# Instance norm on one core: tiles of 48 KiB per partition in four slots, two small parts first and three last

## The chip, the core and the metric

The kernel runs on one core of a Trainium2 chip. Times are device microseconds (us) of the whole program; the profile's span of the same execution is about 1.7 us shorter. The kernel before takes 1248.05 us, the median of three runs (1247.97 to 1248.34). The profile of before is of a run of its own, 1247.95 us.

Engines are named as in the profile: PE is TensorE, DVE is VectorE, ACT is ScalarE, POOL is GpSimd, SP is SyncE. Loads are issued by SP and run in queue q1; stores are issued by ACT and run in queue q10. Both queues run on the same 16 DMA engines.

## The reference

Each of 8 x 64 = 512 instances of 32 x 64 x 64 = 131072 fp32 numbers gets its own mean and variance:

```python
mean = np.mean(x, axis=(2, 3, 4), keepdims=True)
var = np.var(x, axis=(2, 3, 4), keepdims=True)
return ((x - mean) / np.sqrt(var + eps)).astype(np.float32)
```

That is 268.44 MB in and 268.44 MB out, and every number is needed twice on the chip (statistics, then scaling), so each tile stays in SBUF from its load to its store.

## The kernel before

64 tiles of 4 MiB (8 instances, 32 KiB in each of 128 partitions) go through six slots; the last tile is handled as two halves. Per tile, VectorE and ScalarE each sum half, a matmul with a matrix of ones over the partitions of one instance gives the mean, ScalarE squares and sums, a second matmul gives the variance, and the two engines scale half each.

```python
COLS = 8192
SLOTS = 6
FULL = P * COLS // n_elem
ROUNDS = (n_tiles - 1) // SLOTS
...
# on_scalar, per tile
eng.activation(out=unused[:, : 2 * w], in_=t, func=Act.Square,
               bias=a[:, 2:3], accum_out=a[:, 3:4]
)._wait_ge(centred[lane], c1).then_inc(squared[lane], 1)
...
eng.dma_start(out=dst, in_=t)._wait_ge(done[lane], c2).then_inc(stored[lane], 16)
...
# load_all, in the loop: a slot is loaded when its store is through
eng.dma_start(out=slots[s][:], in_=x_t[it * SLOTS + s])._wait_ge(
    stored[s], c16
).then_inc(landed[s], 16)
```

(Cuts are marked with "...".)

## Time and profile before

| what | value | where it is read |
|---|---|---|
| time | 1248.05 us | median of 3 |
| span | 1246.2 us | page |
| DMA queues q1 and q10 | 50.0% and 49.9% of 16 engines' span | page, part 3 |
| ScalarE, VectorE | 79%, 38% | page, part 1 |
| first data packet starts | 2.1 us | packet records |
| idle time of a DMA engine between first and last byte, mean of 16 | 2.1 us | packet records |

The trace has a record of every DMA packet, with start, duration, bytes and queue. A row of one partition is one packet. Packets of one engine follow each other with an overlap of 3 to 4 ns, so they can be chained into 16 engines; where fewer than 16 packets run, an engine is idle. The GB/s of the page count a packet where it starts, so they swing by some per cent from slice to slice; spread over their durations the packets give a flat rate. A packet is called late when its record is over 50 ns longer than the median of its size. The record names no engine, and the chaining is not always unique, so what is said of single engines is good to a packet or two.

### The profile page before, as it was taken

Reading aid. Unit: us, or ns where it says so; the run is one execution under the profiler, and the core shown is the slowest. Engines: PE = TensorE matmul, PEld = TensorE weight load, DVE = VectorE, ACT = ScalarE, POOL = GpSimd, SP = SyncE. Lnnn points to the kernel's source line nnn. Section 1 sums busy time; section 2 is a strip of 40 time slices with the busy share of each in tenths; the row PEclk is TensorE's granted clock in tenths of the full one; section 3 lists DMA queues with packets and bytes.
Section 4 is the critical chain, followed back from the end, with each engine's and each line's share of the span. In section 5 each row is a group of like instructions: output and inputs, shape, how many; then the busy total and the mean of one; then the engine's idle time right before and its main releaser. Section 6 shows DMA issues by size and latency. Waiting matters only on the chain.

```text
span 1246.2 us, 1808 instructions
## 1 busy us (share of the span) xinstructions
PE 76.4 (6%) x260; PEld 65.2 (5%) x260; DVE 468.0 (38%) x325; ACT 986.1 (79%) x410; POOL 1.9 (0%) x11
## 2 busy tenths in 40 slices
PE   0000000000000000000000000000000000000000
PEld 0000000000000000000000000000000000000000
DVE  2344334433334334343343433434334333343331
ACT  5888888887787878778777877787787778878774
POOL 0000000000000000000000000000000000000000
DMA  9999999999999999999999999999999999999998
GB/s 404 421 438 428 430 438 436 428 431 438 435 429 431 438 435 429 431 436 436 429 431 436 436 429 430 438 436 426 433 438 436 426 433 438 435 425 435 438 429 380
DMA packets 18722, 536.90 MB, mean 431 GB/s; under 512 B 2080, under 2 KB 2080, under 8 KB 2080
## 3 DMA queue, kind: packets, MB, share of 16 engines
q1 hardware_dynamic: 9360, 268.44, 50.0%
q10 hardware_dynamic: 9360, 268.44, 49.9%
q14 instruction: 2, 0.02, 0.0%
HBM read 268.44 MB, written 268.44 MB: 431 GB/s over the span
## 4 chain that ended last, share of the span: by engine, by line
ACT 48%; DVE 29%; another core or an unknown queue 13%; PE 6%; issue 1%; DMA 1%; ACTq 0%; DVEq 0%; SPq 0%
ACT unused L113 37%; DVE small L79 18%; DVE slot L95 8%; ACT slot L123 4%; ACT unused L107 4%; PE psum L136 3%; PE psum L143 3%; ACT small L120 1%; ACT L120 1%; DMA slot<-in_x_dram 1%; DVE small L89 1%; DVE small L82 1%; DVE small L92 1%; ACTq L130 0%
## 5 line engine op out<-in xcount | busy, mean ns | idle before, releaser
L113 ACT ACTIVATE unused<-slot,small 128x8192 uint8<-128x8192 f32 (+1 forms) x65 | 456.1, 7016 | 90.2 <-DVE small L82 90.2
L79 DVE TENSOR_REDUCE small<-slot 128x1 f32<-128x4096 f32 (+1 forms) x65 | 283.0, 4353 | 163.7 <-DMA slot<-in_x_dram 163.7
L107 ACT ACTIVATE unused<-slot 128x4096 uint8<-128x4096 f32 (+1 forms) x65 | 231.7, 3564 | 81.9 <-DMA slot<-in_x_dram 76.7
L123 ACT ACTIVATE slot<-slot,small 128x4096 f32<-128x4096 f32 (+1 forms) x65 | 243.7, 3749 | 27.6 <-DVE small L92 27.6
L89 DVE RECIPROCAL small<-small 128x1 f32<-128x1 f32 x65 | 10.6, 164 | 533.8 <-ACT small L120 533.8
L95 DVE TENSOR_SCALAR slot<-slot,small 128x4096 f32<-128x4096 f32 (+1 forms) x65 | 154.7, 2380 | 2.4
L136 PE MATMUL psum<-small,avg 128*128 128x2 f32 x130 | 38.2, 363 | 673.9 <-DVE small L79 548.5
L136 PEld LDWEIGHTS psum<-small,avg 128*128 128x128 f32 x130 | 32.6, 311 | 679.4 <-DVE small L79 552.7
L143 PE MATMUL psum<-small,avg 128*128 128x1 f32 x130 | 38.2, 363 | 480.6 <-ACT unused L113 480.6
L143 PEld LDWEIGHTS psum<-small,avg 128*128 128x128 f32 x130 | 32.7, 312 | 486.1 <-ACT unused L113 486.1
L120 ACT ACTIVATE small<-psum,eps_t 128x1 f32<-128x1 f32 x65 | 17.0, 261 | 37.4 <-PE psum L143 37.3
L82 DVE TENSOR_REDUCE small<-psum 128x1 f32<-128x2 f32 x65 | 10.4, 160 | 62.8 <-PE psum L136 62.8
L107 ACT ACT_TABLE_LOAD x10 | 12.8, 1283 | 10.4 <-ACT slot L123 7.1
L120 ACT ACT_TABLE_LOAD x10 | 12.8, 1283 | 0.2
L107 ACT ACTIVATION_READ_ACCUMULATOR unused<-slot 128x1 f32 x65 | 12.1, 186 | 0.0
L113 ACT ACTIVATION_READ_ACCUMULATOR unused<-slot,small 128x1 f32 x65 | 12.1, 186 | 0.0
L92 DVE TENSOR_TENSOR small<-small 128x1 f32<-128x1 f32 x65 | 10.4, 159 | 2.2
L204 POOL TENSOR_SCALAR_AFFINE_SELECT avg<-avg 128x128 f32<-128x128 f32 x4 | 1.3, 324 | 0.3
L201 POOL MEMSET avg<- 128x128 f32 x2 | 0.4, 204 | 0.5 <-SPq L42 0.5
L246 POOL MEMSET const-bfloat16-1.0<- 128x1 bf16 x1 | 0.1, 101 | 0.0
L246 POOL MEMSET const-uint8-127<- 128x1 uint8 x1 | 0.1, 101 | 0.0
L214 POOL MEMSET eps_t<- 128x1 f32 x1 | 0.1, 99 | 0.0
(2 smaller groups left out, 0.2 us busy)
## 6 DMA issues: line engine op xcount, KB each, us to landing
slot<-in_x_dram SPq DMA_DIRECT2D x63, 4096.0 KB, 53.3
out_dram<-slot ACTq DMA_DIRECT2D x63, 4096.0 KB, 45.3
slot<-in_x_dram SPq DMA_DIRECT2D x2, 2048.0 KB, 55.6
out_dram<-slot ACTq DMA_DIRECT2D x2, 2048.0 KB, 14.7
```

Source lines behind the costliest of these rows:

```text
L79: eng.reduce_sum(out=a[:, 0:1], in_=t[:, :w], axis=mybir.AxisListType.X)._wait_ge(landed[lane], c16).then_inc(summed[lane], 1)
L82: eng.tensor_reduce(out=a[:, 2:3], in_=psum[lane][:, 0:2], axis=mybir.AxisListType.X, op=Alu.add, negate=True,)._wait_ge(meaned[lane], c1) ...
L89: eng.reciprocal(out=a[:, 5:6], in_=a[:, 4:5])._wait_ge(rooted[lane], c1).then_inc(scaled[lane], 1)
L92: eng.tensor_mul(out=a[:, 6:7], in0=a[:, 2:3], in1=a[:, 5:6])._wait_ge(scaled[lane], c1).then_inc(shifted[lane], 1)
L95: eng.tensor_scalar(out=t[:, w:], in0=t[:, w:], scalar1=a[:, 5:6], scalar2=a[:, 6:7], op0=Alu.mult, op1=Alu.add,)._wait_ge(shifted[lane], ...
L107: eng.activation(out=unused[:, w : 2 * w], in_=t[:, w:], func=Act.Identity, accum_out=a[:, 1:2],)._wait_ge(landed[lane], c16).then_inc(sum ...
L113: eng.activation(out=unused[:, : 2 * w], in_=t, func=Act.Square, bias=a[:, 2:3], accum_out=a[:, 3:4],)._wait_ge(centred[lane], c1).then_in ...
L120: eng.activation(out=a[:, 4:5], in_=psum[lane][:, 2:3], func=Act.Sqrt, bias=eps_t[:, 0:1])._wait_ge(varied[lane], c1).then_inc(rooted[lane ...
L123: eng.activation(out=t[:, :w], in_=t[:, :w], func=Act.Identity, scale=a[:, 5:6], bias=a[:, 6:7],)._wait_ge(shifted[lane], c1).then_inc(don ...
L136: eng.matmul(out=psum[lane][:, 0:2], lhsT=avg[n][:], rhs=a[:, 0:2], start=True, stop=True,)._wait_ge(summed[lane], c2).then_inc(meaned[lan ...
L143: eng.matmul(out=psum[lane][:, 2:3], lhsT=avg[n][:], rhs=a[:, 3:4], start=True, stop=True,)._wait_ge(squared[lane], c1).then_inc(varied[la ...
L204: eng.affine_select(out=m[:], in_=m[:], pattern=[[sign * split, n], [0, split]], compare_op=Alu.is_ge, fill=0.0, base=0 if sign < 0 else s ...
```

## The change

The intent: longer rows, so fewer packets and transfers, and shorter ends. A tile now has 48 KiB per partition and holds 12 instances, and there are four slots (4 x 48 = 6 x 32 KiB). 41 such tiles are preceded by two parts of 2 MiB (16 KiB per partition, FRONT) and followed by three. The last three parts use the slot of tile 37 and are loaded when that is stored. The store of the last tile, tile 40, is held until the second of the last three parts has landed. A partition now holds parts of up to two instances' chunks, so sums are kept per third of a tile and brought to instances with masks (four small VectorE operations around each matmul). VectorE takes over the square and sum of one third. The wait of tile 40's store is called the hold below.

```diff
-    COLS = 8192
-    SLOTS = 6
+    CHUNK = 4096
+    THIRDS = 3
+    COLS = THIRDS * CHUNK
+    SLOTS = 4
+    PART = P * CHUNK // n_elem
+    FRONT = 2
+    n_tiles = (n_inst // PART - FRONT) // THIRDS - 1
+    n_parts = n_inst // PART - THIRDS * n_tiles
...
+        eng.tensor_tensor_reduce(
+            out=unused[2][:], in0=chunk[0], in1=chunk[0],
+            scale=1.0, scalar=0.0, op0=Alu.mult, op1=Alu.add,
+            accum_out=column(a, SQUARES, 0),
+        )._wait_ge(moved[lane], c1).then_inc(squared[lane], 1)
...
+        if behind is not None:
+            eng.wait_ge(landed[behind], 16)
+        eng.dma_start(out=dst, in_=t)._wait_ge(done[lane], c3).then_inc(
+            stored[lane], 16
+        )
...
+    AHEAD = SLOTS + n_parts - 2
...
+            if with_target and k == n_tiles - 1:
+                more += (AHEAD,)
...
+    nc.scalar.preload_act_table(Act.Sqrt)
```

## The prediction

> **What bounds the kernel now.** I read the page from the totals down: busy shares, slices, queues, groups, then the waits of the load queue, and last the timeline of the two ends.
>
> ```profile
> PE 76.4 (6%) x260; PEld 65.2 (5%) x260; DVE 468.0 (38%) x325; ACT 986.1 (79%) x410; POOL 1.9 (0%) x11
> DMA  9999999999999999999999999999999999999998
> GB/s 404 421 438 428 430 438 436 428 431 438 435 429 431 438 435 429 431 436 436 429 431 436 436 429 430 438 436 426 433 438 436 426 433 438 435 425 435 438 429 380
> DMA packets 18722, 536.90 MB, mean 431 GB/s; under 512 B 2080, under 2 KB 2080, under 8 KB 2080
> q1 hardware_dynamic: 9360, 268.44, 50.0%
> q10 hardware_dynamic: 9360, 268.44, 49.9%
> ...
> slot<-in_x_dram SPq DMA_DIRECT2D x63, 4096.0 KB, 53.3
> out_dram<-slot ACTq DMA_DIRECT2D x63, 4096.0 KB, 45.3
> ```
>
> No compute engine is full: ScalarE is at 79%. The 16 DMA engines are: nine tenths or more in every slice but the last, and the load queue (q1) and the store queue (q10) fill 50.0% and 49.9% of their time. A tile moves 4 MiB in and 4 MiB out, and at 431 GB/s that takes 8.39 MB / 431 = 19.5 us. A load lands 53.3 us after its issue and a store 45.3 us, which are 2.7 and 2.3 such periods: each queue always holds a transfer behind the running one. ScalarE needs only 7.12 + 3.62 + 3.80 + about 0.9 = 15.4 us of the 19.5.
>
> ```profile
> SPq L185 <- DMA out_dram<-slot: 1048.9, 54, 50.6
> ```
>
> This is the load queue's own wait: loads wait for stores to free slots. It looks like the loss, but costs nothing while earlier loads are still queued, which the 53.3 us say. The chain of waits names ScalarE for 48% for the same reason: it follows semaphores and does not see that the DMA engines are full.
>
> The ends:
>
> ```profile
> 1.03 2.93 SPq L180 DMA_DIRECT2D slot<-in_x_dram  x6
> 13.23 4.42 DVE L79 TENSOR_REDUCE small<-slot 128x1 f32<-128x4096 f32 x1 [13.23 <-DMA slot<-in_x_dram]
> ...
> 1211.81 0.34 ACTq L130 DMA_DIRECT2D out_dram<-slot  x1
> 1222.36 0.34 ACTq L130 DMA_DIRECT2D out_dram<-slot  x1
> 1223.26 1.91 ACT L107 ACTIVATE unused<-slot 128x2048 uint8<-128x2048 f32 x1 [0.93 <-DMA slot<-in_x_dram]
> 1233.70 0.34 ACTq L130 DMA_DIRECT2D out_dram<-slot  x1
> ```
>
> The first 4 MiB land at 13.23; 4.19 MB at 433 GB/s are 9.7 us, so bytes flow from about 3.6 us on. At the end the last half tile lands at 1223.26 and its store is issued 10.4 us later, but earlier stores are still moving: I spread every packet of the trace over its duration and found 16 engines busy in every 2 us bin from 1204 to the end. **Neither end has a hole to close.** The only losses are 3.6 us before the first byte, slow first packets of loads and stores (together 1.5 us per engine), and what a packet costs beyond its bytes.
>
> **What the Trainium skill says.** "DMA: Bandwidth & Descriptors", section "Where 436 GB/s comes from", puts the fabric's ceiling at 435.2 GB/s. The spread packets give 433.2 GB/s over each tenth of the middle: 0.5% below it, so it agrees, and there is no more to win than that half per cent plus the ends. The same page, "Why small descriptors are slow (HBM only)", says that each packet has a small fixed overhead. The packet records agree: 32 KiB take 1213 ns, 16 KiB 611 ns, and twice 611 less 1213 leaves 9 ns; the 4-byte packets that report completion take 9 ns as well. "VectorE: DVE Perf Modes", section "The perf-mode tier table (the rule you actually need)", has tensor_reduce and fp32 tensor_tensor at one element per cycle and fp32 tensor_scalar at two. The trace has 4.42 us for a reduction of 4096 and 2.41 us for the scaling of 4096, so it agrees; I use it to size the new square-and-sum on VectorE. "ScalarE: Activation LUTs", section "What ACT_TABLE_LOAD costs", gives about 1283 ns a load; the page of before has 20 loads of 1283 ns.
>
> **The change part by part.**
>
> *Transfers.* 63 tiles of 4 MiB and two halves become 41 tiles of 6 MiB (48 KiB per partition) and five parts of 2 MiB, two first and three last. Bytes are equal. Per engine, data packets go from (63 + 2) x 8 x 2 = 1040 to (41 + 5) x 8 x 2 = 736, if a 48 KiB row stays one packet as the 32 KiB row does, and completions from 130 to 92. That is 1170 - 828 = 342 fewer. At 9 ns each it is 3.1 us. But neighbouring packets overlap slightly (the durations sum to 16.04 busy engines): at 433.2 GB/s an engine takes 1210.3 ns for 32 KiB, against 1204 ns for the bytes alone (twice the difference of the two sizes), so 6.3 ns for 9/8 of a packet, 5.6 ns each: 342 x 5.6 = **1.9 us**. I take 2.3 us, between the two and nearer the lower.
>
> *VectorE per tile.* Two reductions, 4.42 and about 1.75 (the step from 2282 ns at 2048 to 4419 at 4096 is 1.04 ns an element; 1536 elements); subtracting the mean 2.41; square and sum, estimated from the tier table as a one-element-a-cycle pass at 4.42 plus 0.19 for reading the accumulator; two scalings 4.82; ten small operations of about 0.17. Sum 19.7 us.
>
> *ScalarE per tile.* Sums over 4096 and 2560 elements 3.62 + 2.34, squares 2 x 3.71, scaling 3.80, root 0.26, four accumulator reads 0.75. Sum 18.2 us.
>
> Both lie beside a transfer period of 12.58 MB / 433.2 = 29.0 us. VectorE goes from 38% to about 68%, ScalarE from 79% to about 62%; neither is the bound, so moving work between them is worth nothing in time. All table loads but one go, 19 x 1.28 = 24 us of ScalarE, hidden too.
>
> *Latency of a tile,* landing to store: sums 6.35; masks, matmul and gathering 1.5 (four small operations of 0.2 and a matmul of 0.6); squares 7.8; masks again 1.5; root, reciprocal, shift 0.7; scaling 4.85. Sum 22.7 us, against about 17.4 in before. A slot comes round every 4 x 29.0 = 116 us, leaving 93 us for its load and store, which need 29 each when they share the engines. So both queues stay filled: I expect about 48 us issue to landing for loads and 45 for stores.
>
> *Start.* Part 0 lands near 8.5 us, its store goes out near 19 (10.5 us a part, as the halves in before), is through by about 31, and frees the load of tile 2 near 32. The loads before it are 16 MiB, which with the two small stores last until about 52. No hole. Stores begin 12 us earlier than in before (31.57), but that only reorders bytes: loads already filled the engines.
>
> *End.* Counted from the landing of tile 40: its store is ready at 23; the parts land at 10, 19 and 29, so the hold until the second landed barely waits. Parts compute one after another at about 10.6 us each: stores issued near 34, 45 and 55. Stores already queued last until 34 (tile 39), then 14.5 for tile 40 and 4.8 for each of two parts: 58. The last store's data start about 1.5 us after issue, near 57: covered by about 1 us. I count no hole, but the margin is thin.
>
> *Sum.* 1248.05 - 2.3 = 1245.75; I say **1245.7 us**.
>
> **Rivals.**
> - *A hole at the end.* The margin of 1 us rests on steady queues; if the store backlog is shorter, the engines idle 1 to 4 us before the last parts. For it: 10.6 us a part against 4.8 us of transfer. Against: 6 MiB of tile 40 ahead. Time 1247 to 1249.
> - *Rows of 48 KiB are cut* into 32 + 16 KiB. Then the two data packets of a row cost one fixed part more, and 41 x 128 x 2 / 16 = 656 packets come back per engine: net 314 more than before, +1.8 us, 1250. Nothing in the profile shows a row above 32 KiB; 16 and 32 KiB were both uncut.
> - *VectorE becomes the bound.* It would need the square-and-sum at over three times my estimate (9 us of slack). It would have to exceed 29 us a tile; 30 us would make 41 us more. Unlikely, as known rows make up 15 of the 19.7 us.
> - *Everything hidden, nothing gained.* If the 9 ns overlap wholly with the next packet's reading, only noise is left: 1248.
>
> **Range and chances.** The best case is all 3.1 us and about 1 us at the ends, 1244; the worst likely one a hole of 3 us with little won, 1248.5. I give 1243.7 to 1248.5 for 8 in 10. Over 2% faster would need 1223, below bytes over the ceiling (536.87 MB / 435.2 = 1233.6): 0.01. Over 2% slower needs 1273, a compute-bound or starving loop: 0.03. Within 2%: 0.96.
>
> **What would show it.** Right: DMA nines in all slices, data packets of 48 KiB at about 1815 ns, packets down to about 828 x 16 = 13,250, mean near 432 GB/s, VectorE near 68% and ScalarE near 62%, loads landing after about 48 us and stores after 45, one table load. Wrong: a slice under nine after the first stores or in the last three; packets of 16 KiB at over 1280; a load queue whose wait for stores ends after the previous load landed; a square-and-sum much over 4.6 us; or a per-byte rate that changes with the row length.

## The result, and the profile after

The changed kernel takes **1252.14 us** (median of 4 runs, 1251.42 to 1254.22) beside 1248.14 us of the kernel before: ratio 1.0035, interval 1.0017 to 1.0052. The change is within 2%, as the chances said, but it loses 4 us where 2.3 were to be won, and lies above the range.

The page of the changed kernel, in the same order as for the kernel before:

```profile
PE 55.0 (4%) x184; PEld 46.1 (4%) x184; DVE 804.4 (64%) x722; ACT 764.6 (61%) x441; POOL 2.7 (0%) x15
...
DMA  9999999999999999999999999999999999999997
GB/s 393 427 444 434 427 429 447 430 427 433 444 429 427 446 432 427 433 438 433 429 440 435 432 427 443 435 429 432 441 433 427 440 436 430 430 438 435 433 397 306
DMA packets 13250, 536.89 MB, mean 429 GB/s; under 512 B 1472, under 2 KB 1472, under 8 KB 1472
...
q1 hardware_dynamic: 6624, 268.44, 49.7%
q10 hardware_dynamic: 6624, 268.44, 49.6%
...
L173 DVE CUSTOM_DVE_ANT_0 unused<-slot 128x4096 uint8<-128x4096 f32 x41 | 181.5, 4426 | 1.4
...
slot<-in_x_dram SPq DMA_DIRECT2D x41, 6144.0 KB, 39.9
out_dram<-slot ACTq DMA_DIRECT2D x41, 6144.0 KB, 54.3
slot<-in_x_dram SPq DMA_DIRECT2D x5, 2048.0 KB, 31.6
```

Neither compute engine is the bound (64% and 61%), the packets are as few as predicted, and the DMA row is nines to the last slice. The loss shows in two places only: the last two GB/s figures, 397 and 306 where before had 429 and 380, and the split of the waiting, 39.9 us for a load and 54.3 us for a store.

The timeline of the last 75 us, cut to the last tile and the parts; a bracket is idle time of the engine and what ended it:

```profile
1178.01 3.62 ACT L215 ACTIVATE unused<-slot 128x4096 uint8<-128x4096 f32 x1 [8.27 <-DMA slot<-in_x_dram]
...
1197.46 2.40 DVE L202 TENSOR_SCALAR slot<-slot,small 128x4096 f32<-128x4096 f32 x1
...
1213.28 0.35 ACTq L244 DMA_DIRECT2D out_dram<-slot  x1
1213.67 1.91 ACT L290 ACTIVATE unused<-slot 128x2048 uint8<-128x2048 f32 x1 [14.56 <-DMA slot<-in_x_dram]
...
1223.84 0.35 ACTq L310 DMA_DIRECT2D out_dram<-slot  x1
...
1234.40 0.34 ACTq L310 DMA_DIRECT2D out_dram<-slot  x1
...
1244.95 0.34 ACTq L310 DMA_DIRECT2D out_dram<-slot  x1
```

Tile 40 lands at 1178.0 and is ready at 1199.9, but its store goes out at 1213.28: the hold lasts 13.4 us, and ScalarE, which issues stores, stands still with it (14.56 us), though part 2 has landed near 1199. The three parts then follow at 10.6 us each. The stretches of 10 us at the end; the last two figures of a line are the share of the DMA engines and GB/s. First before, then after:

```profile
1220.00:1230.00 10.00, 0.59 (x2) 0.50 (x2) 3.95 (x5) 7.68 (x4) 0.00 (x0) 1.00 0.98 421
1230.00:1240.00 10.00, 0.59 (x2) 0.50 (x2) 1.67 (x3) 2.57 (x4) 0.00 (x0) 1.00 0.98 421
```

```profile
1220.00:1230.00 10.00, 1.18 (x4) 1.00 (x4) 4.02 (x5) 7.60 (x7) 0.00 (x0) 1.00 0.88 380
1230.00:1240.00 10.00, 1.17 (x4) 1.00 (x4) 4.02 (x5) 7.61 (x7) 0.00 (x0) 1.00 0.86 364
1240.00:1250.00 10.00, 0.59 (x2) 0.50 (x2) 1.67 (x3) 3.81 (x4) 0.00 (x0) 1.00 0.45 188
```

The DMA engines run dry between the parts' stores. They do so once before tile 40's store as well: spread packets give 5.7 busy engines at 1212 to 1214, and 0.1 to 2.6 at 1240 to 1246. The packet records give 8.9 us of idle time per engine after, 2.1 before; the difference of 6.8 us is slightly more than the difference of the spans, 6.3. So in this run all of the loss is idle time, and about 0.5 us was won elsewhere. It is the slowest of the four runs (1254.22 us); the others left no trace.

Two things in the packet records explain where this comes from, and became the theories.

**Shares by packet.** The last three loads were to take 9.7 us each, half of the engines. They took 20.0, 13.3 and 12.0 us. While tile stores ran beside them, loads moved about 105 GB/s and stores 320. That is the ratio of the rows: 16 KiB in a load packet, 48 KiB in a store packet. The Trainium skill has the rule behind it in "DMA: Bandwidth & Descriptors", section "Queues, rings and completion order": each engine goes round its queues one packet at a time. The traces agree, with one row as the packet: in the middle of before, over 99% of an engine's records are followed by one of the other queue. Equal numbers of packets give bytes in the ratio 1 to 3, and 433 / 4 = 108 GB/s for the loads. **The trace of before had shown it too**: its two last half tiles, 16 KiB rows beside 32 KiB stores, took 14.0 us each, where half the engines would have needed 9.7 and a third needs 14.5.

**Late loads.** In the middle of the run before (about 50 to 1170 us of the span), one of some 14,800 data packets took over 50 ns more than the median of its size. After, 24 did, by 59 to 536 ns, 23 of them loads, and some 15 of them fell to two engines. In sum they are 6.0 us late, 0.4 us per engine. A tile counts as landed only when all 16 engines have reported: the reports of one transfer drift apart slowly in before, to 2.1 us at the end; in after they lie 2.4 us apart through most of the middle, 3.7 at tile 40, and up to 9.6 in the last loads. The changed kernel's runs also spread by 2.8 us where those of before spread by 0.4 (in later rounds a few runs of before came in up to 1250.3).

### The profile page after: what moved, and what is told of

It is laid out like the page before. It is cut to its first block, busy times and chain, and to the rows that moved or that the text cites. A ratio compares the mean times of both kernels' runs of the same rounds, so it can differ in the third digit from the quotient of the medians.

```text
span 1252.5 us, 1978 instructions
## 1 busy us (share of the span) xinstructions
PE 55.0 (4%) x184; PEld 46.1 (4%) x184; DVE 804.4 (64%) x722; ACT 764.6 (61%) x441; POOL 2.7 (0%) x15
## 2 busy tenths in 40 slices
DMA packets 13250, 536.89 MB, mean 429 GB/s; under 512 B 1472, under 2 KB 1472, under 8 KB 1472
## 4 chain that ended last, share of the span: by engine, by line
another core or an unknown queue 82%; DMA 10%; ACT 4%; DVE 2%; SPq 1%; issue 1%; PE 0%; ACTq 0%
DMA slot<-in_x_dram 6%; DMA out_dram<-slot 4%; ACT unused L222 1%; SPq L390 1%; ACT unused L293 1%; ACT slot L303 1%; DVE small L159 0%; ACT unused L215 0%; ACT unused L290 0%; DVE slot L202 0%; DVE slot L195 0%; PE psum L254 0%; PE psum L319 0%; PE psum L316 0%
## 5 line engine op out<-in xcount | busy, mean ns | idle before, releaser
L215 ACT ACTIVATE unused<-slot 128x4096 uint8<-128x4096 f32 x82 | 243.4, 2968 | 304.0 <-DMA slot<-in_x_dram 301.7
L159 DVE TENSOR_REDUCE small<-slot 128x1 f32<-128x4096 f32 x82 | 249.3, 3082 | 274.0 <-DMA slot<-in_x_dram 274.0
L222 ACT ACTIVATE unused<-slot,small 128x4096 uint8<-128x4096 f32 x82 | 303.4, 3701 | 63.7 <-DVE small L145 63.7
L173 DVE CUSTOM_DVE_ANT_0 unused<-slot 128x4096 uint8<-128x4096 f32 x41 | 181.5, 4426 | 1.4
L235 ACT ACTIVATE slot<-slot,small 128x4096 f32<-128x4096 f32 x41 | 155.9, 3802 | 18.1 <-DVE small L190 18.1
L202 DVE TENSOR_SCALAR slot<-slot,small 128x4096 f32<-128x4096 f32 x41 | 98.7, 2407 | 0.0
L254 PE MATMUL psum<-small,avg 128*128 128x9 f32 (+1 forms) x164 | 49.1, 375 | 1118.0 <-DVE small L127 1118.0
L166 DVE TENSOR_SCALAR slot<-slot,small 128x4096 f32<-128x4096 f32 x41 | 96.5, 2353 | 1.5
L195 DVE TENSOR_SCALAR slot<-slot,small 128x4096 f32<-128x4096 f32 x41 | 96.2, 2347 | 0.0
L254 PEld LDWEIGHTS psum<-small,avg 128*128 128x128 f32 x164 | 41.1, 311 | 1126.0 <-DVE small L127 1126.0
L127 DVE TENSOR_TENSOR small<-small,belongs 128x12 f32<-128x12 f32 x82 | 13.9, 170 | 31.2 <-ACT unused L222 28.8
L293 ACT ACTIVATE unused<-slot,small 128x4096 uint8<-128x4096 f32 x5 | 18.5, 3707 | 4.6 <-DVE small L270 4.6
L267 DVE TENSOR_REDUCE small<-slot 128x1 f32<-128x2048 f32 x5 | 11.4, 2281 | 8.7 <-DMA slot<-in_x_dram 8.7
L139 DVE TENSOR_TENSOR small<-small,belongs 128x9 f32<-128x9 f32 x82 | 13.9, 170 | 2.8
L222 ACT ACTIVATION_READ_ACCUMULATOR unused<-slot,small 128x1 f32 x82 | 15.3, 187 | 0.0
L215 ACT ACTIVATION_READ_ACCUMULATOR unused<-slot 128x1 f32 x82 | 15.3, 187 | 0.0
L145 DVE TENSOR_REDUCE small<-small 128x3 f32<-128x9 f32 x82 | 13.3, 162 | 2.8
## 6 DMA issues: line engine op xcount, KB each, us to landing
slot<-in_x_dram SPq DMA_DIRECT2D x41, 6144.0 KB, 39.9
out_dram<-slot ACTq DMA_DIRECT2D x41, 6144.0 KB, 54.3
```

The costliest lines, as they stand in the source:

```text
L127: eng.tensor_tensor(out=block(a, by_both, n, m), in0=spread(a, at, m), in1=belongs[:, :, :m], op=Alu.mult,)._wait_ge(*wait).then_inc(steps ...
L139: eng.tensor_tensor(out=block(a, by_chunk, n, n), in0=spread(a, by_instance, n), in1=belongs[:, :, :n].rearrange("p i c -> p c i"), op=Alu ...
L159: eng.reduce_sum(out=column(a, SUMS, j), in_=part, axis=AXIS)._wait_ge(landed[lane], c16).then_inc(summed[lane], 1)
L166: eng.tensor_scalar(out=chunk[0], in0=chunk[0], scalar1=column(a, MEANS, 0), scalar2=None, op0=Alu.add,)._wait_ge(centred[lane], c1).then_ ...
L173: eng.tensor_tensor_reduce(out=unused[2][:], in0=chunk[0], in1=chunk[0], scale=1.0, scalar=0.0, op0=Alu.mult, op1=Alu.add, accum_out=colum ...
L195: eng.tensor_scalar(out=chunk[0], in0=chunk[0], scalar1=column(a, SCALES, 0), scalar2=None, op0=Alu.mult,)._wait_ge(scaled[lane], c1).then ...
```

## The experiments

The stated theory: unequal rows starve the last loads, which makes the hold long and the engines run dry; late loads of 48 KiB rows add to it. Rival 1: the hold alone does it. Rival 2: three parts of 10.6 us each behind 4.8 us transfers do it. Further rivals concern the late loads: address pitch, first parts, or length of the packets.

The table has all runs; "late" counts packets of the middle over 50 ns late, "idle" is the mean idle time of an engine between first and last byte; both are of the traced run.

| kernel | us, median (range, runs) | late | idle us |
|---|---|---|---|
| before | 1248.05 (1247.97 to 1248.34, 3) | 1 | 2.1 |
| changed | 1252.14 (1251.42 to 1254.22, 4) | 24 | 8.9 |
| e1, no hold | 1255.26 (1253.57 to 1260.93, 6) | 70 | 7.9 |
| e2, last stores in 16 KiB rows | 1250.75 (1247.32 to 1258.57, 6) | 29 | 2.3 |
| e3, last tile's store behind the loads | 1251.91 (1248.10 to 1253.94, 6) | 44 | 8.4 |
| e4, no last parts | 1248.92 (1246.89 to 1251.03, 5) | 40 | 4.3 |
| e5, before with half rows | 1255.42 (1255.31 to 1255.59, 4) | 1 | 4.1 |
| e6, all tiles in 16 KiB rows | 1255.65 (1254.48 to 1256.12, 4) | 2 | 4.2 |
| e7, no first parts | 1249.80 (1247.76 to 1257.26, 5) | 101 | 10.8 |
| e8, e6 with 4 KiB rows for the last loads | 1260.70 (1258.58 to 1262.79, 4) | 2 | 8.4 |
| e9, e6 without the hold | 1255.62 (1254.21 to 1255.76, 4) | 2 | 4.1 |
| e10, e8 without the hold | 1267.06 (1265.75 to 1267.45, 4) | 2 | 15.3 |
| e11, only stores in 16 KiB rows | 1291.72 (1288.92 to 1293.06, 4) | 973 | 26.3 |
| e12, only loads in 16 KiB rows | 1289.91 (1286.24 to 1294.95, 4) | 875 | 23.7 |
| e13, all tiles in 24 KiB rows | 1250.45 (1250.15 to 1250.75, 4) | 2 | 2.6 |

Runs of before beside them had medians of 1247.93 to 1248.22. All results were correct.

### e1: the hold taken away

```diff
-            if with_target and k == n_tiles - 1:
-                more += (AHEAD,)
```

> The store of tile 40 no longer waits for the landing of the second last part. Theory (engines share by packet, so 16 KiB load rows get a quarter beside 48 KiB store rows): the parts' loads go on at about 108 GB/s under the store of tile 40, the last part lands near 1233 instead of 1221, time 1250 to 1255, no gain. Rival 1 (the hold alone makes the holes): holes go, 1245 to 1246. Rival 2 (three parts of 10.6 us each after 4.8 us transfers): stores of the parts issued about 13 us earlier, 1245 to 1247.

Measured: 1255.26 us, ratio to before 1.0063 (1.0046 to 1.0080). The trace shows the theory's picture: the store of tile 40 goes out at 1199.1, and beside it the second and third of the last loads take 19.2 and 18.5 us. The last lands at 1234.2 and its store is issued at 1244.65, only 0.3 us earlier than in the changed kernel (1244.95). Rival 1 falls: without the hold nothing is won. Rival 2 falls as well in its simple form, since the parts' loads, not their compute, set the pace here: ScalarE waits 7 us for each of the last two.

### e2: the last stores in rows of 16 KiB

```diff
-    ROUNDS = n_tiles // SLOTS
+    ROUNDS = n_tiles // SLOTS - 1      # so tiles 36 to 40 stand outside the loop
...
+        w = COLS // pieces             # 3 for tiles 38, 39 and 40, else 1
+        for i in range(pieces):
+            eng.dma_start(out=dst[:, i * w : (i + 1) * w], in_=t[:, i * w : (i + 1) * w]) ...
```

> Tiles 38, 39 and 40 are stored as three transfers of 16 KiB rows each; hold and parts stay. Theory: loads of the parts now get half of the engines, 9.7 us each instead of 20.0, 13.3 and 12.0; the hold ends within 2 us of the tile's own work; the last store is issued near 1233; holes under 2 us; 1244.5 to 1247. Rival 1: hold is still there, so holes of several us stay, 1249 or more. Rival 2: three parts one after another still end late, holes stay, 1249 or more.

The traced run did what the theory expected. Its timeline, cut to the issues of the last stores:

```profile
1194.90 1.43 ACTq L247 DMA_DIRECT2D out_dram<-slot  x3
...
1206.54 0.34 ACTq L313 DMA_DIRECT2D out_dram<-slot  x1
...
1217.08 0.34 ACTq L313 DMA_DIRECT2D out_dram<-slot  x1
...
1227.63 0.34 ACTq L313 DMA_DIRECT2D out_dram<-slot  x1
```

and its stretches at the end:

```profile
1220.00:1230.00 10.00, 0.70 (x3) 0.52 (x3) 1.83 (x4) 6.16 (x4) 0.00 (x0) 1.00 1.01 431
1230.00:1240.00 10.00, 0.00 (x0) 0.00 (x0) 0.00 (x0) 0.00 (x0) 0.00 (x0) 1.00 1.01 433
```

The loads took 10.5, 10.3 and 10.6 us, tile 40 was stored as soon as it was ready, and the DMA share stays at 1.01. The last three parts still follow each other at 10.5 us, without a hole: rival 2 is refuted for equal rows. The span was 1245.6 us, 0.6 less than before's. But the other runs took 1249.6 to 1258.6 us: only the traced run, at 1247.32, came near the expected 1244.5 to 1247, and 29 loads were late even there. With the end mended, something that varies from run to run is left.

### e3: the last tile's store behind the loads, in their queue

```diff
-        if behind is not None:
-            eng.wait_ge(landed[behind], 16)
+        # tile 40: not stored by ScalarE; in load_all, after the last part's load:
+        eng.dma_start(out=out_t[k], in_=slots[k % SLOTS][:])._wait_ge(
+            done[k % SLOTS], 3 * (k // SLOTS + 1)
+        ).then_inc(stored[k % SLOTS], 16)
```

> The store of tile 40 is issued on the load queue behind the parts' loads, so it is still behind them but ScalarE does not stand still for it. Theory: parts land as late as before (rows of 16 KiB beside 48 KiB), but part 2 is computed from about 1200, its store goes out near 1211, the last near 1233, all under the 6 MiB of tile 40; holes under 2 us, 1244.5 to 1247. Rival 1: the same. Rival 2: holes at the end stay, 1249 or more.

A miss: 1251.91 us. ScalarE no longer stood still (the first part's store was issued at 1214.1, the last at 1237.5 instead of 1244.95), yet the program ended no earlier. The packet records name the reason in the traced run: 14 of the 16 engines moved their last byte within 1.2 us of each other, one 3.6 us and one 7.3 us after the first of them; 44 packets of the middle had been late, and the 16 reports of one transfer mostly lay 5.9 us apart there. The time of such a run is set by its slowest engine.

### e4: no parts at the end, and e7: no parts at the start

```diff
# e4: 42 tiles, two parts first, none last
-    n_tiles = (n_inst // PART - FRONT) // THIRDS - 1
+    n_tiles = (n_inst // PART - FRONT) // THIRDS
# e7: 42 tiles, no parts first, two last
-    FRONT = 2
+    FRONT = 0
-    n_tiles = (n_inst // PART - FRONT) // THIRDS - 1
+    n_tiles = n_inst // PART // THIRDS
```

> 42 tiles and no parts at the end; the two first parts stay. Theory: no 16 KiB rows beside 48 KiB rows at the end; the last tile's store is issued 22.7 us after its landing while about 24 us of stores are queued: hole about 1 us, 1245 to 1248. Rival that the large tiles or the first parts cost the time: 1251 to 1253 as the changed kernel.

> 42 tiles from the first byte, then two parts at the end; no parts first. If the first parts (16 KiB packets that put the engines out of step, and a base shifted by 4 MiB) make the late packets, the middle has none over 50 ns and engines stay within 2 us of each other: 1246 to 1248. If the 48 KiB rows do, late loads stay and runs spread by several us: 1248 to 1256.

e4 took 1248.92 us, ratio 1.0002 (0.9989 to 1.0015): undoing the last parts alone gives back what the change had lost, though its median is 1 us above what was expected and 40 loads were late. So the large tiles and the first parts show no loss or gain against before, within a spread of 4 us. Its trace has a hole of its own, though: the engines run dry from 1226 to 1231, before the last store, issued at 1229.81. e7 took 1249.80 us with runs from 1247.76 to 1257.26, and 101 packets late: the first parts do not make the late loads. Its two last parts were starved like those of the changed kernel (20.6 and 23.9 us), and its traced run, the slowest, has 10.8 us of idle time; yet its other four runs took 1247.76 to 1249.96 us. What a starved end costs thus varies from run to run.

### e5: the kernel before with rows half as long

```diff
-        eng.dma_start(out=dst, in_=t)._wait_ge(done[lane], c2).then_inc(stored[lane], 16)
+        for i in range(2):                       # loads likewise; counts 32 instead of 16
+            eng.dma_start(out=dst[:, i * w : (i + 1) * w], in_=t[:, i * w : (i + 1) * w]) ...
```

> The kernel before with every transfer cut in two, rows of 16 KiB instead of 32 (8 instead of 16 for the halves): 1170 more packets per engine. If a packet costs its 9 ns less the 3.5 ns by which neighbours overlap, 5.5 ns, it takes 6.4 us more, 1254.6; at 9 ns 10.5 us, 1258.7; if packet costs are hidden, 1248. No packet of the middle over 50 ns late, as in before.

1255.42 beside 1247.93 us: 7.5 us for 1170 packets per engine, 6.4 ns each. That lies between the two expectations, nearer the lower one. So the packet cost that the prediction rested on is real; its 2.3 us for 342 packets is 6.7 ns each. Not all of the 7.5 us is packet cost, however: 2.0 us are idle time (4.1 against 2.1), as one engine moved its last byte 3.7 us after the first one to end (2.0 in before). The middle's rate, 431.2 GB/s beside 433.2, accounts for 5.7 us, 4.8 ns a packet. Rows of 16 KiB are not late (1 packet).

### e6: the changed kernel with all tiles in rows of 16 KiB; e13: in rows of 24 KiB

```diff
-        eng.dma_start(out=dst, in_=t)._wait_ge(done[lane], c3).then_inc(stored[lane], 16)
+        for i in range(THIRDS):                  # e13: range(2), halves; loads likewise
+            w = slice(i * CHUNK, (i + 1) * CHUNK)
+            eng.dma_start(out=dst[:, w], in_=t[:, w])._wait_ge(done[lane], c3).then_inc(
+                stored[lane], 16
+            )
```

> The changed kernel with every tile moved as three transfers of 16 KiB rows, at the same addresses. Two theories of the late packets (loads of single engines, 100 to 700 ns late in the middle): a row of 48 KiB in one packet makes them, then none is left over 50 ns in the middle, all runs lie within 1 us, and the time is 1245.5 plus 1476 more packets at 5.5 ns, 1253.6; the addresses or the pitch make them, then they stay, with a spread of several us between runs and 1255 to 1262. Shares are equal, so the last parts load in 9.7 us each and the hold ends within 2 us of the tile's work under both.

> Every tile moved as two transfers of 24 KiB rows, loads and stores alike. If only packets well above 32 KiB are late, none is over 50 ns in the middle, runs agree within 1.5 us, and with 396 more packets than the kernel before at 6.4 ns (2.5 us) the time is 1250 to 1252.5. If the pitch of 48 KiB counts, late packets stay and runs spread: 1252 to 1258.

Addresses, slots, tiles, parts, masks and hold are the same as in the changed kernel; only the packets are shorter. The late loads are gone in both (2 packets each), and runs agree within 1.7 and 0.6 us. Both times are those of the packet count: e6 has 1134 packets per engine more than before and takes 7.7 us more, 6.8 ns each; e13 has 396 more and takes 2.4 us more, 6.0 ns each. (These figures, too, hold some idle time at the end; the middle's rates, 431.2 and 432.5 GB/s, give 5.1 and 4.9 ns.) e5, which has rows of the same length in the kernel before, stands 0.2 us below e6. So **everything else in the change costs nothing and gains nothing** that these runs can show, and the late loads belong to the 48 KiB packets, not to the pitch. In e6 the last parts loaded in 10.3, 10.3 and 12.3 us, and tile 40 was stored as soon as it was ready, as expected with equal shares. e13 is the fastest form of the change that is steady:

```profile
GB/s 386 436 429 433 434 430 434 434 430 435 431 431 437 431 430 437 431 431 436 431 433 434 430 434 433 431 435 431 431 437 431 430 438 430 431 435 431 432 434 370
DMA packets 25058, 536.90 MB, mean 430 GB/s; under 512 B 2784, under 2 KB 2784, under 8 KB 2784
```

The last two slices are back at 434 and 370 (the changed kernel had 397 and 306), with the hold and the three last parts in place, because a load row of 16 KiB beside store rows of 24 KiB gets two fifths instead of a quarter: its last parts took 12.3, 12.0 and 12.8 us, where two fifths of 433 GB/s need 12.1.

### e8, e9, e10: shares and hold, apart, without late loads

To test the shares where nothing is late, e6 was taken as the base: e8 loads the last three parts in rows of 4 KiB, which get a fifth beside 16 KiB stores; e9 takes the hold out of e6, e10 out of e8.

```diff
+            for i in range(n):                   # e8 and e10: n = 4 for the last parts
+                w = slice(i * CHUNK // n, (i + 1) * CHUNK // n)
+                load = eng.dma_start(out=t[:, w], in_=part_of(x_f, m)[:, w])
...
-            if with_target and k == n_tiles - 1:   # e9 and e10
-                more += (AHEAD,)
```

> As the kernel with all tiles in 16 KiB rows (1255.65 us, no late packets), but the last three parts are loaded in rows of 4 KiB. Only their share beside the stores changes, from a half to a fifth, 87 GB/s or 24 us each, and 135 more packets cost 0.9 us. If shares by packet make the holes of the changed kernel, the hold is long again and 5 to 12 us of idle engines appear: 1261 to 1268. If late packets or the hold alone made them, 1256 to 1257.

> As the kernel with all tiles in 16 KiB rows (1255.65 us), without the hold. With equal shares the hold costs and gives little: within 1 us of it. If the hold alone costs several us, 1250 to 1253.

> Rows of 4 KiB for the last loads and no hold. If shares by packet make the holes, taking the hold away does not help, since the store of tile 40 then takes four fifths of the engines from the last loads: 1262 to 1275. If the hold is the cause, 1256 to 1257.

| us, median | hold | no hold |
|---|---|---|
| equal rows, 16 and 16 KiB | 1255.65 (e6) | 1255.62 (e9) |
| unequal rows, 4 and 16 KiB | 1260.70 (e8) | 1267.06 (e10) |

With equal rows the hold does nothing. With unequal rows the end costs 5.1 us with the hold and 11.4 without (0.5 of it estimated for the extra packets, 81 by 6.4 ns; the 135 of the expectation were miscounted). So the shares make the holes, and the hold halves them: it is the remedy, not the cause. e8 came in slightly below the 1261 to 1268 expected of the theory; its first part loaded in 24.6 us, against the 24 worked out, and its tile 40 was stored 8.4 us later than e6's.

### e11, e12: only the stores, or only the loads, in rows of 16 KiB

```diff
# e11: the store loop of e6, loads unchanged
# e12: the load loop of e6, stores unchanged
```

> The changed kernel with loads in 48 KiB rows, but every store of a tile in three transfers of 16 KiB rows. If long load packets alone make the late loads, they stay (more than ten over 50 ns in the middle) and runs spread by several us, 1250 to 1258. If late loads need long store packets beside them, none is left and runs agree within 1 us near 1250. Engines divide the last loads and stores evenly, so the last parts land as in the thirds kernel.

> The counterpart of the kernel with only the stores cut: loads of tiles in three transfers of 16 KiB rows, stores in rows of 48 KiB. If long load packets make the late loads, none over 50 ns is left in the middle and runs agree within 1 us; 697 more packets at 6.4 ns are 4.5 us on top of 1245.5, plus the tail with its quarter share, 1250 to 1256. If unequal packets of loads and stores make them (as with the stores cut, 1292 us), many late packets again and over 1265.

Both were a surprise: 1291.72 and 1289.91 us, 3.4% and 3.3% slower than before, where e11's expectation had 1250 to 1258 and the better-behaved branch of e12's had 1250 to 1256. The page of e11:

```profile
GB/s 388 440 424 430 427 420 416 426 429 433 418 422 430 420 426 429 425 422 431 435 429 428 429 422 428 427 420 439 421 428 423 422 424 425 423 425 417 410 324 172
DMA packets 25058, 536.90 MB, mean 416 GB/s; under 512 B 2784, under 2 KB 2784, under 8 KB 2784
...
out_dram<-slot ACTq DMA_DIRECT2D x128, 2048.0 KB, 45.2
slot<-in_x_dram SPq DMA_DIRECT2D x41, 6144.0 KB, 25.0
```

It has the same packet count as e13 and 41 us more time: 16 us per engine are the late packets themselves, and 24 us more are idle time (26.3 against 2.6). 973 packets of the middle were late, 260 us in sum, and the 16 reports of one transfer came up to 57 us apart; e12 is alike (875, 295 us, 53 us). The shares show in the waits as well: in e11 a 6 MiB load needs 25.0 us, in e12 a store of that size 24.2, against 54.3 for a store of the changed kernel. Mixing 16 and 48 KiB packets for whole tiles is thus far worse than either alone. A simple "long loads are late" doesn't explain it: in e12 the loads are short and 554 of them were late.

What stays open: why these packets are late at all. Shown is only that they need packets of 48 KiB in at least one direction at this pitch, that they are mostly loads in the changed kernel, and that mixing lengths multiplies them.

## Why the prediction was wrong

- **What bounds it: right.** The DMA engines were full through the middle, 433.7 GB/s spread over the packets' durations (433.2 before), and no compute change mattered: e13 and e6 lie on the packet count.
- **The packet cost: right in kind, somewhat too large.** 48 KiB rows stayed whole at 1815 ns and the packets are 13,250 as said. The prediction took 6.7 ns a packet, between its 9 and 5.6; the rates of the middle in e5, e6 and e13 give 4.8 to 5.1, which is 1.7 us for 342. The middle's rate rose by 0.1%, which is some 1.4 us of the 2.3.
- **Engine loads: right.** The square and sum took 4.43 us (4.42 estimated), VectorE 64% (68%), ScalarE 61% (62%), one table load. The tile's latency was 21.9 us (22.7).
- **The end: the step that failed.** "The parts land at 10, 19 and 29, so the hold until the second landed barely waits" took half the engines for loads. The term is the transfer time of a last part: 9.7 us predicted; 20.0, 13.3 and 12.0 measured. With it the parts landed about 21, 35 and 44 us after tile 40, the hold lasted 13.4 us, and 6.8 us more idle time came. Of the hold, up to 5.7 us are the engines' being out of step: so far apart lay the 16 reports of the part that it waited for. The first rival, a hole at the end, named the right place but for a wrong reason and too small: the store backlog was not short, as tile 39's store landed 33 us after tile 40's load, with 34 predicted. The trace of before had the evidence: 14.0 us for 2 MiB beside longer rows.
- **A step that was missing.** The prediction named "a per-byte rate that changes with the row length" as what would make it wrong, and gave it no size. Single 48 KiB packets were late, engines fell out of step, and runs spread. It was not in the rivals or the range. Why such packets are late stays open.
- **Start and waits: partly wrong.** Half shares were assumed for the first stores as well; the first took 16.9 us instead of 9.7. The waits came out at 39.9 us for loads and 54.3 for stores instead of 48 and 45. That the unequal first rows set this split is not shown: e7, with no first parts, has 35.1 and 59.1. Neither cost time in the middle, as the engines stayed full.
- **Two readings of before: slightly off.** The packet records have the first data packets start at 2.1 us; they take 1.7 to 2.2 us, and the 3.6 us worked back from the landing counts this slowness in. And not all 16 engines are busy to the end: from 1242 to 1244 us 8 are on average, and after that one or none. Most of the 2.1 us of idle time lies there. The sum of the prediction does not rest on either.

How the 6.4 us between 1245.7 and 1252.14 divide is not settled. A first estimate takes e4, which has late loads and no starved parts and stands at 1248.92: about 3 us for the late loads and 3 for the end. But e4's own 4.3 us of idle time include a hole before its last store, e7 was starved at its end and mostly ran near 1249, and late packets by themselves are 0.4 us per engine, so that they cost more only by putting the engines out of step. Runs of these kernels overlap by several us. None of the versions measured beats the kernel before; e4 is equal to it.

## What to carry to other kernels

When two queues share the DMA engines, count packets, not bytes: the queue with the shorter rows got the smaller part here (105 GB/s of 16 KiB rows beside 320 of 48 KiB), and a small last load beside large stores can take twice as long as its size says. Before shortening a program's last pieces, give both directions rows of equal length there, or look in the existing trace at what a short-row transfer beside a long-row one really took. Once the engines are full, longer rows win only nanoseconds per packet (about 5 ns here, under 0.2% of the time for 342 packets an engine), so weigh what a new row length does to the steadiness of the single engines, over several runs.

## What the Trainium skill lacked or had wrong

- "DMA: Bandwidth & Descriptors" has the round of one packet per queue, but not its consequence for unequal rows: 16 KiB loads beside 48 KiB stores got 105 of about 430 GB/s, and mixing the two lengths throughout cost 3.3 to 3.4% (1290 and 1292 us). It gives 9 to 17 descriptors as typical of a packet; here the turn was a single row, with over 99% of the records in the middle of before followed by one of the other queue.
- The same page prefers packets of at most 4096 B for software-generated descriptors and says nothing of how steadily long rows run on these queues. Here a packet record is a whole row of up to 48 KiB. With tile rows of one length, 16, 24 and 32 KiB were steady (1 or 2 late packets a run), 48 KiB was not (24 to 101).
- The same page gives a packet's fixed overhead in cycles (about 3), but no time for it on these queues. The runs show 4.8 to 5.1 ns per packet and engine by the rate of the middle, and 6.0 to 6.8 ns of the program's time, the idle time at the end included.
